# Opening of a streaming-encoder layer: the second half's squares, scales and weight sums moved in a hand-written order, one product taken in whole words for three groups, the first taps later

## Chip, cores and metric

One core of one Trainium2 chip runs the whole layer in one launch. The metric is device microseconds of one execution, median of several. TensorE (PE) does the matrix products, VectorE (DVE) and ScalarE (ACT) prepare their operands and empty their results, GpSimd (POOL) takes a few additions, SyncE (SP) issues most of the transfers.

## The reference, cut to what matters

```
mod = silu(c) @ ada_w + ada_b                      # six rows of 1024: shift, scale, gate, twice
h   = rms_norm(x, g0) * (1 + sc_m) + sh_m          # x: 2048 x 1024, float32
bcv = h @ w_in                                     # 1024 x 3072 -> gate_b, gate_c, v
u   = gate_c * v;  conv = 3 causal taps of u
h   = (gate_b * conv) @ w_out
x   = x + g_m * rms_norm(h, g1)
h   = rms_norm(x, g2) * (1 + sc_f) + sh_f
x   = x + g_f * rms_norm((silu(h@w_g) * (h@w_u)) @ w_down, g3)
```

All is float32. The change lies in the first lines alone: the norm, the modulation and the start of `h @ w_in`.

## The kernel before

**Products.** Every matrix product goes through a Strassen-Winograd step: seven block products P1 to P7 take the place of eight. Their moving operands are built from four quarters of the normalized x, all 128 x 2048: `a` and `b` (tokens 0 to 511, lower and upper half of the channels), `c` and `d` (tokens 512 to 1023). A11 = a (for P1), A12 = b (P2), S3 = e = a - c (P7), S2 = d - e (P6), S1 = c + d (P5), S4 = b - S2 (P3), A22 = d (P4). The stationary operands are 128 x 512 blocks of the weight or sums of two or three of them (`Blocks.sum`).

**Split words.** A float32 operand is split in two fp32r words: ACT casts the high one (`high`, `upper`), DVE subtracts it from the whole to get the low one (`low`, `lower`). One block of 128 contracted channels (a `k`; four to a product) is then three matmuls of 128x512: wh·hi, wl·hi, wh·lo. Below, "a triple".

**Slots.** A phase is a list of slots, one product of one group each (`resident`). In the first phase, in0, groups n = 0, 1, 2 are c, C and b of the first quarter of the channels (gate_c, v and gate_b in the reference come from them); slots 0 to 4 are P1 of n = 0 to 4, 5 to 9 P2 of n = 0 to 4, 10 to 12 P7, 13 to 15 P6, 16 to 18 P5, 19 to 21 P3 and 22 to 24 P4 of n = 0 to 2; then 25 P6, 26 P7, 27 P5 and 28 P3 of n = 3, and so on with n = 4 beside it.

**Order.** Each engine works its instructions in the order in which the program emits them. From slot 13 on a loop emits them slot by slot: `supply` brings weights so many slots ahead (blocks 9, sums 7, high 5, low 4), `events` hold the steps of features, `later(x, f)` puts f x slots on. Slots 0 to 12 are the opening, `start()`, written out by hand: loads of everything first, then the norm factors (`squares`, `factor`/`root`, `spread`, which multiplies by a matrix of ones on PE and copies the result to `rb`), the modulation vectors (`scales`, `shifts`, `turned`, `fold`), the features (`mult` on DVE, `shift` and `upper` on ACT, `lower` on DVE), the products (`products`) and what follows one (`follow`: after P1 an ACT copy c11, after P2 a DVE sum). In the trace's names A12h and A12l are high and low word of A12, r1 is the norm factor of the second 512 tokens, xr their rows of x, v, r1p and r1t steps of its root, in0P a bank of PSUM (left of the arrow) and in3P a pair of weight words (right).

**Accumulators.** A group's P1, P6, P5 and P3 add up in one PSUM bank `pa`, read between them: c11 after P1 and c21 after P6 and c22 after P5, each an ACT copy. So P5 of a group can't start until the copy c21 is through. `taps` (one ACT product and two DVE multiply-adds) and `ready_b` (two DVE products, then `sums` and stores) follow once P3 and P4 of the three groups are there.

**Buffers.** 17 tiles of 128 x 2048 (`big`), 16 raw blocks, 7 weight pairs, 10 temporaries, 8 PSUM banks.

Of the kernel before, what the change touches and what calls it, by code (L numbers as in the profile page):

```python
# [15 lines left out]
P = 128  # L16
# [6 lines left out]
EPS = 1e-6  # L23
# [2 lines left out]
SUBS = ((0, 4), (4, 4), (8, 3))  # L26

LEAD = 3

EARLY = 5  # L30

# [16 lines left out]
def hybrid_conv_layer(  # L48
# [17 lines left out]
    class Engine:  # L66


        def __init__(self, engine):
            self.engine = engine  # L70
# [24 lines left out]
    def pair(name):  # L95
        return pairs.tile([P, 2, CH], F32, tag="wp", bufs=NWP, name=name)
# [306 lines left out]
    class Weight:  # L403


        def __init__(self, kind, grp, op, of, keep=False, ks=None):
            self.kind, self.grp, self.op, self.of, self.keep = kind, grp, op, of, keep
            self.key = (kind, grp, op)
            self.n = width(kind, grp)
            if ks:  # L410
                self.n = len(ks) * P
                self.of = Single(kind, grp, slice(ks[0] * P, (ks[-1] + 1) * P))
            elif of:
                of.split[op] = self
# [16 lines left out]
        def high(self):  # L431
            if self.of:
                self.t = self.of.operand(self.op)
                self.w = pair(f"{self.kind}{self.grp}{self.op}")
                A.copy(self.w[:, 0, : self.n].bitcast(F32R), self.t)

        def low(self):
            if self.of:
                w, n = self.w, self.n
                V.tensor_tensor(w[:, 1, :n].bitcast(F32R), self.t, w[:, 0, :n], ALU.subtract)  # L440
                if self.keep:
                    kept[self.key] = scratch([P, 2, CH], f"k{self.kind}{self.grp}{self.op}")
                    later(2, lambda: A.dma_start(kept[self.key][:, :, :n], w[:, :, :n]))
# [55 lines left out]
    class Group:  # L499
# [72 lines left out]
        def taps(self, u, j, pos):  # L572
            ph = self.ph
            if self.i not in ph.y:
                ph.y[self.i] = big(f"{ph.name}y{self.i}")
            t = ph.y[self.i][:, pos, :]
            w = lambda tap: col(vt, VW + tap * KD + j)

            def rest():
                V.scalar_tensor_tensor(t, u[:, 1 : CH + 1], w(1), t, ALU.mult, ALU.add)  # L580
                V.scalar_tensor_tensor(t, u[:, 0:CH], w(0), t, ALU.mult, ALU.add)

            lag = 0.5 if self.n < LEAD else 1.5
            later(lag, lambda: A.activation(t, u[:, 2:], AF.Copy, scale=w(2)))
            later(lag + (0.5 if self.n < LEAD else 1), rest)

        def ready_b(self, c):
            ph = self.ph
            if c == "12":
                both = (0, self.c11), (2, self.pa)  # L590
            elif c == "21":
                both = (1, self.c21), (3, self.c22)
            else:
                return
            t = ph.y[self.i]
            for pos, src in both:
                V.tensor_tensor(t[:, pos, :], src, t[:, pos, :], ALU.mult)
            own = self.n == len(ph.groups) - 1 and stay[ph.u]
            if c == "12":
                for op, pos in ("A11", 0), ("A12", 2):  # L600
                    if own:
                        later(0.5, partial(own[op][0], t[:, pos, :]))
                        later(1, partial(own[op][1], t[:, pos, :]))
                    else:
                        later(1, partial(store_operands, y_d[ph.u], self.i, (op, t[:, pos, :])))
            if {"12", "21"} <= self.done:
                run(sums(t, y_d[ph.u], self.i, f"{self.name}s", own))


# [259 lines left out]
    for s in slots:  # L869
        ph = s.ph  # L870
        if ph.kind in ("out", "down"):
            w = Weight(ph.kind, s.grp, s.op, None, ks=s.ks)
        elif s.n < LEAD and ph.name != "in0" or ph.name == "in1" and s.g.i == 2:
            w = Weight(ph.kind, s.grp, s.op, None)
        else:
            b = of.setdefault((ph.name, s.n), Blocks(ph.kind, s.grp))
            w = Weight(ph.kind, s.grp, s.op, b, ph.name == "in0" and s.g.i in (1, 2))
        s.w = w
        position.append(len(order))
        order.append(w)  # L880
        if s.n >= LEAD and extra.get(ph.name) and len(position) > 7 * LEAD + 2 * (EARLY - LEAD):
            n = count[ph.name] = count.get(ph.name, 0) + 1
            total = 7 * (len(ph.groups) - LEAD)
            every = 7 * len(in_between[ph.name])
            while extra[ph.name] and every - len(extra[ph.name]) < (0.6 * n if n < total / 3 else n * every / (total - 6)):
                order.append(extra[ph.name].pop(0))
# [7 lines left out]
    def advance(step, to):  # L894
        st = steps[step]
        while st[0] <= to:
            if step in BEFORE:
                advance(BEFORE[step], st[0])
            getattr(order[st[0]], step)()
            st[0] += 1  # L900
# [151 lines left out]
    def start():  # L1052
# [81 lines left out]
        def products(first, ks, ns=range(3)):  # L1134
            for k in ks:
                for n in ns:
                    multiply(slots[first + n], (k,), follow=False)
# [30 lines left out]
        def split(key, op, ks):  # L1168
            for k in ks:
                shift(key, k)  # L1170
                upper(op, k)
                lower(op, k)
# [50 lines left out]
        advance("high", 7)  # L1223
        products(4, range(2, 4), range(1))
        advance("low", 7)
        fold(2)
        shifts(3)
        split("b", "A12", range(2))
        squares(1, range(2, 4))
        dg = factor(1, lambda: [scales(3, i) for i in range(2)])  # L1230
        products(5, range(2), range(1))
        turned(3)
        fold(3)
        follow(0, range(3))
        products(6, range(2), range(1))
        rb[1] = spread(dg, "r1")
        split("b", "A12", range(2, 4))
        products(5, range(2, 4), range(2))
        follow(3, range(2))
        advance("high", 8)  # L1240
        advance("low", 8)
        for k in range(4):
            mult("c", k)
            shift("c", k)
        products(7, range(4), range(1))
        follow(5, range(2))
        advance("high", 9)
        advance("low", 9)
        advance("sums", 12)
        products(8, range(4), range(2))  # L1250


        f.t["e"] = big(f"{ph.name}e")
# [2 lines left out]
            V.tensor_tensor(f.t["e"][:, k, :], f.t["a"][:, k, :], f.t["c"][:, k, :], ALU.subtract)  # L1256
            upper("S3", k)

        for k in range(4):
            e(k)  # L1260
            if k:
                advance("low", 9 + k)
                lower("S3", k - 1)
            if k < 3:
                advance("high", 10 + k)
            if k == 1:
                follow(7, range(1))
            if k == 3:
                follow(8, range(2))
        lower("S3", 3)  # L1270
        products(10, range(2))
        products(10, range(2, 4))
# [15 lines left out]
        follow(10)  # L1288


        for k in range(4):
            V.tensor_tensor(f.t["c"][:, k, :], f.t["c"][:, k, :], f.t["d"][:, k, :], ALU.add)
            upper("S1", k)
        advance("sums", 18)
        advance("high", 18)
        for k in range(4):
            lower("S1", k)
        advance("low", 18)
        for i, step in ((14, f.s4), (15, partial(f.high, "S4")), (16, partial(f.low, "S4")),
                        (17, partial(f.high, "A22")), (18, partial(f.low, "A22"))):  # L1300
            schedule(i, step)

    for ph in phases[1:]:
# [34 lines left out]
    def multiply(s, ks=None, follow=True):  # L1338
        g, op = s.g, s.op
        ks = ks or s.ks  # L1340
        if s.first and op in ("P1", "P2", "P7") and ks[0] == 0:
            t = bank(f"{s.ph.name}{op}_{s.n}")
            setattr(g, {"P1": "pa", "P2": "pb", "P7": "pd"}[op], t)
        acc = {"P2": "pb", "P7": "pd", "P4": "pd"}.get(op, "pa")
        acc = getattr(g, acc)
        hi, lo = s.ph.A[FEATURES[op], s.key]
        begin = s.first and op in ("P1", "P2", "P7")
        last = s.last and ks[-1] == s.ks[-1]
        for k in ks:
            c = slice((k - s.ks[0]) * P, (k - s.ks[0] + 1) * P)  # L1350
            wh, wl = s.w.w[:, 0, c].bitcast(F32R), s.w.w[:, 1, c].bitcast(F32R)
            PE.matmul(acc, wh, hi[:, k, :], start=begin and k == 0, stop=False, skip_group_check=True)
            PE.matmul(acc, wl, hi[:, k, :], start=False, stop=False, skip_group_check=True)
            PE.matmul(acc, wh, lo[:, k, :], start=False, stop=last and k == ks[-1], skip_group_check=True)
        if last and follow:
            g.after(op)
# [64 lines left out]
```

## Time and profile before

| | |
|---|---|
| time, median of 3 runs | 1998.7 us (1995.0 to 1999.45) |
| the profiled execution, its own time | 1995.86 us |
| its span, first to last instruction | 1994.1 us |
| PE busy in the span | 1946.8 us (98%), 8472 matmuls |
| DVE busy | 1467.3 us (74%) |
| ACT busy | 871.1 us (44%) |
| mean granted TensorE clock | 0.992 of full |

The busy share of PE is a mean over the whole run; matmuls are pipelined and their ends are modelled, so a stretch at 10.00 us of 10 is a stretch without a wait, at the clock that was granted in it. The opening has to be read by itself, from the timelines of its engines.

### The profile page before, as it was taken

Reading aid. Unit: us, or ns where it says so; the run is one execution under the profiler, and the core shown is the slowest. Engines: PE = TensorE matmul, PEld = TensorE weight load, DVE = VectorE, ACT = ScalarE, POOL = GpSimd, SP = SyncE. Lnnn points to the kernel's source line nnn. Section 1 sums busy time; section 2 is a strip of 40 time slices with the busy share of each in tenths; the row PEclk is TensorE's granted clock in tenths of the full one; section 3 lists DMA queues with packets and bytes.
Section 4 is the critical chain, followed back from the end, with each engine's and each line's share of the span. In section 5 each row is a group of like instructions: output and inputs, shape, how many; then the busy total and the mean of one; then the engine's idle time right before and its main releaser. Section 6 shows DMA issues by size and latency. Waiting matters only on the chain.

```text
span 1994.1 us, 25033 instructions
## 1 busy us (share of the span) xinstructions
PE 1946.8 (98%) x8472; PEld 1580.3 (79%) x8472; DVE 1467.3 (74%) x2165; ACT 871.1 (44%) x1434; POOL 345.2 (17%) x224
## 2 busy tenths in 40 slices
PE   7799998999999999999999999999999999999998
PEld 3578886777888888888888888888888888888886
DVE  4898778987999876798677755687776665565466
ACT  4533445643434653444333444553333333344452
POOL 0011111310220220144242320120100000011010
PEclk9899999999999999999999999999999999999999
DMA  9349959859996773687566787668565242386644
GB/s 390 119 171 365 330 184 338 308 200 320 313 343 214 288 278 133 195 264 259 180 225 205 262 275 291 230 228 278 184 199 171 101 160 99 106 301 232 198 140 132
DMA packets 204464, 458.98 MB, mean 230 GB/s; under 512 B 22832, under 2 KB 38320, under 8 KB 197936
## 3 DMA queue, kind: packets, MB, share of 16 engines
q1 hardware_dynamic: 176688, 391.98, 57.1%
q10 hardware_dynamic: 27648, 65.41, 8.5%
q8 instruction: 66, 1.08, 0.2%
q14 instruction: 62, 0.51, 0.1%
HBM read 326.23 MB, written 131.07 MB: 229 GB/s over the span
## 4 chain that ended last, share of the span: by engine, by line
PE 73%; DVE 12%; DMA 8%; issue 4%; ACT 2%; ACTq 0%; SPq 0%; POOL 0%; POOLq 0%; DVEq 0%
PE gu1P L76 21%; PE gu0P L76 17%; PE down0P L76 11%; PE down1P L76 9%; PE in0P L76 7%; PE in1P L76 4%; PE out1P L76 4%; DMA ada<-ada_d 1%; DMA in2b<-w_in_d 1%; DVE zz L76 1%; DVE ada L76 1%; DMA kgu0P<-gu0P 1%; DVE xx L76 1%; DVE in1c L76 1%; DVE in0y L76 1%
## 5 line engine op out<-in xcount | busy, mean ns | idle before, releaser
L76 DVE TENSOR_TENSOR gu1a<-gu1P,gu1a 128x512 f32<-128x512 f32 x63 | 43.5, 691 | 108.6 <-PE gu1P L76 108.6
L76 DVE TENSOR_TENSOR gu0a<-gu0P,gu0a 128x512 f32<-128x512 f32 x63 | 43.3, 688 | 71.9 <-PE gu0P L76 69.5
L76 POOL TENSOR_TENSOR gu1a<-gu1a 128x512 f32<-128x512 f32 x11 | 19.0, 1727 | 363.4 <-DVE gu1g11s L76 42.5
L76 POOL TENSOR_TENSOR nq<-nq,nq 128x512 f32<-128x512 f32 x28 | 43.4, 1550 | 144.2 <-ACT nq L76 135.3
L76 ACT COPY gu1a<-gu1P 128x512 f32<-128x512 f32 x42 | 24.7, 588 | 98.6 <-PE gu1P L76 87.4
L76 ACT COPY gu0a<-gu0P 128x512 f32<-128x512 f32 x42 | 24.5, 587 | 84.0 <-PE gu0P L76 82.9
L76 DVE CUSTOM_DVE_ANT_0 ada<-ada,c 128x512 f32<-128x512 f32 x80 | 58.9, 747 | 3.0 <-DMA ada<-ada_d 3.0
L76 ACT COPY gu1g<-gu1P 128x512 f32<-128x512 f32 x24 | 14.1, 589 | 92.9 <-PE gu1P L76 92.9
L76 POOL TENSOR_TENSOR down0q<-down0q,down0q 128x512 f32<-128x512 f32 x14 | 23.9, 1706 | 144.1 <-ACT down0q L76 144.0
L76 POOL TENSOR_TENSOR gu0a<-gu0a 128x512 f32<-128x512 f32 x11 | 18.2, 1658 | 171.5 <-ACT gu0a L76 47.7
L76 ACT COPY gu0g<-gu0P 128x512 f32<-128x512 f32 x24 | 14.1, 588 | 77.1 <-PE gu0P L76 77.1
L76 POOL TENSOR_TENSOR down1q<-down1q,down1q 128x512 f32<-128x512 f32 x10 | 16.1, 1611 | 148.7 <-ACT down1q L76 148.6
L76 DVE TENSOR_TENSOR gu1g<-gu1P,gu1g 128x512 f32<-128x512 f32 x24 | 16.6, 691 | 27.4 <-ACT gu1g L76 26.0
L76 DVE TENSOR_TENSOR down2P<-down2P,down2P 128x512 fp32r<-128x512 f32 x14 | 12.0, 854 | 28.6 <-ACT down2P L76 28.6
L76 ACT ACTIVATE gu1a<-gu1a 128x512 f32<-128x512 f32 x42 | 26.6, 633 | 13.4 <-DVE xo L76 6.0
L76 POOL TENSOR_TENSOR in0y<-in0y 128x512 f32<-128x512 f32 x4 | 5.9, 1465 | 152.7 <-ACT in4P L76 84.7
L76 ACT ACTIVATE gu0a<-gu0a 128x512 f32<-128x512 f32 x42 | 26.6, 632 | 9.9 <-DVE gu0a L76 8.3
L76 POOL TENSOR_TENSOR out1q<-out1q,out1q 128x512 f32<-128x512 f32 x14 | 22.1, 1580 | 50.4 <-ACT out1q L76 50.4
L76 POOL TENSOR_TENSOR out0q<-out0q,out0q 128x512 f32<-128x512 f32 x14 | 22.7, 1618 | 45.6 <-ACT out0q L76 45.5
L76 DVE TENSOR_TENSOR xx<-xx,zz 128x512 f32<-128x512 f32 x32 | 29.1, 908 | 1.1
L76 ACT ACTIVATE nq<-xx 128x512 f32<-128x512 f32 x32 | 20.2, 632 | 19.1 <-DVE xx L76 18.9
L76 DVE TENSOR_TENSOR gu0g<-gu0P,gu0g 128x512 f32<-128x512 f32 x24 | 16.6, 690 | 14.8 <-ACT gu0g L76 13.3
(3231 smaller groups left out, 6750.0 us busy)
## 6 DMA issues: line engine op xcount, KB each, us to landing
ada<-ada_d SPq DMA_DIRECT2D x64, 256.0 KB, 5.3
act0A<-gu0a SPq DMA_DIRECT2D x33, 256.0 KB, 3.5
act1A<-gu1a SPq DMA_DIRECT2D x33, 256.0 KB, 2.9
ada<-ada_d SPq DMA_DIRECT2D x16, 512.0 KB, 9.4
zz<-z SPq DMA_DIRECT2D x32, 256.0 KB, 5.0
xx<-xt_d SPq DMA_DIRECT2D x32, 256.0 KB, 5.2
x<-xx ACTq DMA_DIRECT2D x32, 256.0 KB, 4.8
down0S<-act0S SPq DMA_DIRECT2D x8, 1024.0 KB, 7.0
```

Of the source, the lines that this page charges most:

```text
L76: return tc.keep_in_program_order(f(*args, **kwargs))
```

## The change

Five edits, all before slot 30.

1. **Squares.** The squares of the last two row blocks of the second 512 tokens stand ahead of the fold of the third quarter and of the first split of `b`, on ACT; before they stood behind the split of two of the four parts of `b`. The root `v` of it follows at once on DVE and POOL.
2. **Scales and sums.** The last two `scales` (DVE) are put between the two splits of `b`, the last `fold` ahead of the diagonal, the weight sums of P7 (`sums` 12) ahead of the second half of `b`, the `mult`s of `c` between its splits.
3. **P2 group by group.** P2 of n = 2, 3 and 4 runs one group after the other; before n = 3 and 4 went together, k by k. The sums that follow P2, the weight words of P7 and the parts of `e` and S3 are dealt out anew around it.
4. **Whole words.** P5 of n = 0, 1, 2 takes `c` (which holds S1 then) and the weight block as they are, float32 times float32, one matmul a `k` in place of three: no split of S1 nor of these three weights in the opening. The other nine groups need S1's words; they are made at slots 22 (high) and 23 (low), each in one instruction of 128x2048. S4's subtraction comes forward from slot 14.
5. **Taps.** For n < 3 the ACT product of the taps is 2 slots later, the DVE part 2 slots too, `ready_b` 3 slots.

```diff
+UNSPLIT = {"P5": "c"}
 ...
     def high(self):
             self.t = self.of.operand(self.op)
+            if self.whole_words:
+                return
 ...
-            lag = 0.5 if self.n < LEAD else 1.5
+            lag = 2.5 if self.n < LEAD else 1.5
 ...
         def ready_b(self, c):
+            if self.n < LEAD:
+                later(3, partial(self.gated, c))
+            else:
+                self.gated(c)
 ...
         advance("low", 7)
+        squares(1, range(2, 4))
         fold(2)
         shifts(3)
-        split("b", "A12", range(2))
-        squares(1, range(2, 4))
-        dg = factor(1, lambda: [scales(3, i) for i in range(2)])
-        products(5, range(2), range(1))
+        v = small(4, "v1")
+        V.tensor_scalar(v, sq[1], EPS, None, ALU.add)
+        steps = root(v, "r1")
+        next(steps)
+        shift("b", 0)
+        upper("A12", 0)
+        scales(3, 0)
+        lower("A12", 0)
+        shift("b", 1)
+        upper("A12", 1)
+        scales(3, 1)
+        dg = at_once(steps)
+        lower("A12", 1)
         turned(3)
         fold(3)
-        follow(0, range(3))
-        products(6, range(2), range(1))
-        rb[1] = spread(dg, "r1")
-        split("b", "A12", range(2, 4))
+        dg = diagonal(dg, "r1")
+        products(5, range(2), range(1))
+        rb[1] = spread(dg, "r1")
+        products(6, range(2), range(1))
+        advance("sums", 12)
+        shift("b", 2)
+        upper("A12", 2)
+        mult("c", 0)
+        lower("A12", 2)
+        mult("c", 1)
+        shift("b", 3)
+        upper("A12", 3)
+        lower("A12", 3)
+        follow(0, range(3))
+        mult("c", 2)
+        mult("c", 3)
         products(5, range(2, 4), range(2))
         follow(3, range(2))
-        advance("high", 8)
+        advance("high", 9)
+        follow(5, range(1))
         advance("low", 8)
+        follow(6, range(1))
+        products(7, range(4), range(1))
         for k in range(4):
-            mult("c", k)
             shift("c", k)
-        products(7, range(4), range(1))
-        follow(5, range(2))
-        advance("high", 9)
         advance("low", 9)
-        advance("sums", 12)
-        products(8, range(4), range(2))
+        products(8, range(4), range(1))
+        follow(7, range(1))
+        products(9, range(4), range(1))
 ...
+        e(0)
+        advance("high", 10)
+        e(1)
+        follow(8, range(1))
+        advance("low", 10)
+        lower("S3", 0)
+        advance("high", 11)
+        advance("low", 11)
+        follow(9, range(1))
+        lower("S3", 1)
+        e(2)
+        advance("high", 12)
+        e(3)
+        advance("low", 12)
+        lower("S3", 2)
         lower("S3", 3)
 ...
+        ph.whole = {op: f.t[key] for op, key in UNSPLIT.items()}
         for k in range(4):
             V.tensor_tensor(f.t["c"][:, k, :], f.t["c"][:, k, :], f.t["d"][:, k, :], ALU.add)
-            upper("S1", k)
-        advance("sums", 18)
+            if k:
+                advance("sums", 15 + k)
         advance("high", 18)
-        for k in range(4):
-            lower("S1", k)
-        advance("low", 18)
-        for i, step in ((14, f.s4), (15, partial(f.high, "S4")), (16, partial(f.low, "S4")),
-                        (17, partial(f.high, "A22")), (18, partial(f.low, "A22"))):
+        f.s4()
+        for i, step in ((15, partial(f.high, "S4")), (16, partial(f.low, "S4")),
+                        (17, partial(f.high, "A22")), (18, partial(f.low, "A22")),
+                        (22, partial(f.high, "S1")), (23, partial(f.low, "S1"))):
 ...
+        if s.w.whole_words:
+            for k in ks:
+                PE.matmul(acc, s.w.t[:, k * P : (k + 1) * P], s.ph.whole[op][:, k, :], start=False,
+                          stop=k == s.ks[-1], skip_group_check=True)
```

## Rows read from the trace of the kernel before

**Rows 1.** Busy time of the engines in stretches of the run: the stretch and its length in us, busy us and (instructions) of PE, PE's weight loads, DVE, ACT, POOL, then the granted TensorE clock, the DMA share and GB/s.

```profile
20.00:30.00 10.00, 7.21 (x29) 3.86 (x29) 8.48 (x24) 5.03 (x8) 0.00 (x0) 1.00 1.03 421
46.00:60.00 14.00, 9.40 (x38) 4.60 (x37) 6.96 (x28) 8.78 (x16) 1.38 (x1) 0.94 0.92 369
60.00:66.00 6.00, 6.00 (x16) 4.67 (x17) 4.52 (x8) 4.61 (x8) 0.00 (x0) 0.57 0.00 0
...
88.00:98.00 10.00, 8.24 (x34) 5.93 (x33) 9.90 (x18) 5.96 (x11) 0.00 (x0) 1.00 0.00 0
98.00:104.00 6.00, 4.72 (x14) 3.75 (x15) 5.84 (x8) 2.29 (x3) 0.00 (x0) 0.72 0.29 87
...
130.00:139.00 9.00, 5.53 (x17) 3.79 (x17) 8.86 (x17) 4.14 (x8) 0.71 (x1) 0.81 0.57 230
139.00:200.00 61.00, 61.00 (x269) 50.47 (x270) 51.48 (x73) 20.45 (x36) 17.68 (x12) 1.00 0.96 361
...
1000.00:1100.00 100.00, 100.00 (x443) 82.81 (x442) 71.98 (x90) 36.07 (x64) 33.95 (x23) 1.00 0.64 220
```

**Rows 2.** The chain of work that ended last, in order of time, of the first 200 us: start us, length us, engine and tile.

```profile
51.99 0.17 DVE v L76
...
138.87 61.31 PE in0P L76 x269
```

**Rows 3.** PE's timeline: start us, length us, then the operation, out<-in, the array used, shape, count, and in brackets the idle time before it and what ended it.

```profile
22.27 0.73 PE L76 MATMUL in0P<-in0A11h,in0P 128*128 128x512 f32 x2 [2.13 <-ACT in0A11h L76]
...
56.57 1.12 PE L76 MATMUL r1b<-r1d,one 128*128 128x512 f32 x2 [2.44 <-DVE mB L76]
59.73 1.22 PE L76 MATMUL in0P<-in0A12h,in0P 128*128 128x512 f32 x2 [2.04 <-ACT in0A12h L76]
...
65.02 0.72 PE L76 MATMUL in0P<-in0A12h,in2P 128*128 128x512 f32 x2
...
77.94 0.71 PE L76 MATMUL in0P<-in0S3h,in1P 128*128 128x512 f32 x2 [3.27 <-DVE in0c L76]
...
90.07 0.39 PE L76 MATMUL in0P<-in0S2l,in0P 128*128 128x512 f32 x1
...
95.51 0.39 PE L76 MATMUL in0P<-in0S2l,in2P 128*128 128x512 f32 x1
97.49 0.51 PE L76 MATMUL in0P<-in0S1h,in0P 128*128 128x512 f32 x1 [1.59 <-ACT in0c L76]
99.28 0.76 PE L76 MATMUL in0P<-in0S1h,in0P 128*128 128x512 f32 x1 [1.29 <-DVE in0P L76]
...
108.97 0.62 PE L76 MATMUL in0P<-in0S4h,in0P 128*128 128x512 f32 x2
...
130.50 0.39 PE L76 MATMUL in0P<-in0S3l,in3P 128*128 128x512 f32 x1
133.69 1.22 PE L76 MATMUL in0P<-in0S1h,in3P 128*128 128x512 f32 x2 [2.79 <-ACT in0c L76]
...
138.87 0.74 PE L76 MATMUL in0P<-in0S4h,in3P 128*128 128x512 f32 x2 [0.68 <-ACT in0c L76]
```

**Rows 4.** ACT's timeline, same columns.

```profile
44.97 0.61 ACT L76 CAST in2P<-in2b 128x512 fp32r<-128x512 f32 x1
...
49.77 1.05 ACT L76 ACTIVATE xr<-xr 128x1024 f32<-128x1024 f32 x1
...
60.43 0.62 ACT L76 CAST in0A12h<-in0b 128x512 fp32r<-128x512 f32 x1
60.95 0.58 ACT L76 COPY in0c<-in0P 128x512 f32<-128x512 f32 x1
...
63.90 2.94 ACT L76 ACTIVATE in0c<-in0c,mB,mA 128x512 f32<-128x512 f32 x4 [1.36 <-DVE in0c L76]
...
131.40 0.72 ACT L76 ACTIVATE in0y<-in0C,vt 128x512 f32<-128x512 f32 x1 [2.43 <-DVE in0C L76]
...
133.06 0.58 ACT L76 COPY in0c<-in0P 128x512 f32<-128x512 f32 x1
```

**Rows 5.** DVE's timeline, same columns.

```profile
72.30 0.68 DVE L76 TENSOR_TENSOR in0S3l<-in0e,in0S3h 128x512 fp32r<-128x512 f32 x1
...
78.91 2.48 DVE L76 TENSOR_TENSOR in0d<-in0d,r1r 128x512 f32<-128x512 f32 x4
...
88.54 1.28 DVE L76 TENSOR_TENSOR in0S2l<-in0a,in0S2h 128x512 fp32r<-128x512 f32 x2
...
92.16 1.41 DVE L76 TENSOR_TENSOR in0b<-in0b,in0b 128x512 f32<-128x512 f32 x2
...
96.14 2.49 DVE L76 TENSOR_TENSOR in0S1l<-in0c,in0S1h 128x512 fp32r<-128x512 f32 x4
...
118.78 1.53 DVE L76 SCALAR_TENSOR_TENSOR in0y<-in0c,vt,in0y 128x512 f32<-128x512 f32 x2
```

**Rows 6.** The weight loads of PE's first six matmuls, float32 times float32, 128x128 by 128x512, two loads to a matmul: start us, length us, what ended the idle time before.

```profile
11.82 0.19 PEld L76 LDWEIGHTS wb<-w,one 128*128 128x128 f32 x1 [0.24 <-issue]
12.25 0.19 PEld L76 LDWEIGHTS wb<-w,one 128*128 128x128 f32 x1 [0.24 <-issue]
```

**Rows 7.** The rows of x for the second factor: SP's issue of their four loads, and the time from issue to landing of all eight loads of rows, least, median and most.

```profile
31.37 3.48 SPq L76 DMA_DIRECT2D xr<-x_d  x4
...
DMA to landing us min/median/max: 4.3/8.6/9.9
```

More of the change, by code (lines that the diff above doesn't have):

```diff
@@ L403, in hybrid_conv_layer, with __init__ @@
     class Weight:
-        def __init__(self, kind, grp, op, of, keep=False, ks=None):
+        def __init__(self, kind, grp, op, of, keep=False, ks=None, whole_words=False):
+            self.whole_words = whole_words
             self.kind, self.grp, self.op, self.of, self.keep = kind, grp, op, of, keep
@@ L437, in low @@
         def low(self):
-            if self.of:
+            if self.of and not self.whole_words:
                 w, n = self.w, self.n
@@ L587, in ready_b, with gated @@
         def ready_b(self, c):
+            if self.n < LEAD:
+                later(3, partial(self.gated, c))
+            else:
+                self.gated(c)
+        def gated(self, c):
             ph = self.ph
@@ L605, in ready_b @@
                         later(1, partial(store_operands, y_d[ph.u], self.i, (op, t[:, pos, :])))
-            if {"12", "21"} <= self.done:
+            self.done.add("gated" + c)
+            if {"gated12", "gated21"} <= self.done:
                 run(sums(t, y_d[ph.u], self.i, f"{self.name}s", own))
@@ L876, in hybrid_conv_layer @@
             b = of.setdefault((ph.name, s.n), Blocks(ph.kind, s.grp))
-            w = Weight(ph.kind, s.grp, s.op, b, ph.name == "in0" and s.g.i in (1, 2))
+            w = Weight(ph.kind, s.grp, s.op, b, ph.name == "in0" and s.g.i in (1, 2),
+                       whole_words=ph.name == "in0" and s.n < LEAD and s.op in UNSPLIT)
         s.w = w
@@ L1257, in e @@
             upper("S3", k)
-        for k in range(4):
[L1260 to L1269, printed above, removed]
+        e(0)
[13 more added lines that the diff above has]
+        lower("S3", 2)
         lower("S3", 3)
@@ L1288, in start @@
         follow(10)
+        ph.whole = {op: f.t[key] for op, key in UNSPLIT.items()}
         for k in range(4):
             V.tensor_tensor(f.t["c"][:, k, :], f.t["c"][:, k, :], f.t["d"][:, k, :], ALU.add)
-            upper("S1", k)
-        advance("sums", 18)
+            if k:
+                advance("sums", 15 + k)
         advance("high", 18)
-        for k in range(4):
-            lower("S1", k)
-        advance("low", 18)
-        for i, step in ((14, f.s4), (15, partial(f.high, "S4")), (16, partial(f.low, "S4")),
-                        (17, partial(f.high, "A22")), (18, partial(f.low, "A22"))):
+        f.s4()
+        for i, step in ((15, partial(f.high, "S4")), (16, partial(f.low, "S4")),
+                        (17, partial(f.high, "A22")), (18, partial(f.low, "A22")),
+                        (22, partial(f.high, "S1")), (23, partial(f.low, "S1"))):
             schedule(i, step)
@@ L1345, in multiply @@
         acc = getattr(g, acc)
+        if s.w.whole_words:
+            for k in ks:
+                PE.matmul(acc, s.w.t[:, k * P : (k + 1) * P], s.ph.whole[op][:, k, :], start=False,
+                          stop=k == s.ks[-1], skip_group_check=True)
+            if follow:
+                g.after(op)
+            return
         hi, lo = s.ph.A[FEATURES[op], s.key]
```

## The prediction

> **What bounds the kernel now.** I read the stretches first. Late in the run PE is busy for 100.00 us of 100 at full clock, and from 139 us on for 61.00 of 61 [rows 1]; the chain of waits has one unbroken piece of PE there [rows 2]. So beyond 139 us an instruction on DVE or ACT costs nothing, and whatever brings 138.87 forward brings the end forward, as far as PE's work beyond stays the same. Ahead of it PE loses time in two ways: it stands idle, and after idle stretches it runs at a lower clock (a mean of 0.57 in 60 to 66, 0.72 in 98 to 104, 0.81 in 130 to 139) [rows 1]. Then I read PE's timeline for the places: ahead of r1b and of the second half of P2 (2.44 and 2.04 idle), in P7 (3.27), at the start of P5 (1.59 and 1.29), at P5 of group 3 (2.79), at P3 of group 3 (0.68) [rows 3]. Last I read what DVE and ACT did there: from 78 to 98 DVE is busy for nearly all of the stretch, so there the order and number of DVE's instructions set the time, and PE merely follows [rows 1].
>
> Prices. A triple at full clock: P6 of n = 1 and 2, eight triples, from 90.30 (the start of the triple behind the one at 90.07) to about 95.74 is 5.44, so 0.68 each. At the low clock: four triples from 59.73 to 65.02, 1.32 each. Small DVE work of 128x512 follows itself every 0.60 to 0.62 (the four of 2.48 at 78.91), ACT casts every 0.52, shifts every 0.73, copies every 0.48 (60.95 and its neighbours, an estimate from their 0.58 less the overlap seen in the four shifts) [rows 3 to 5].
>
> **Term 1, from the squares to S3: 6.0 us.** The chain of waits runs through v at 51.99 [rows 2], which waits for ACT's two last squares, behind the two splits of b, at 49.77 [rows 4]. The squares now follow the cast of 44.97 at 45.5. Their rows are there: the last of four issues is out by 34.85, and the longest landing of rows took 9.9, so 44.8 [rows 7]. Two squares with their sums take 2.1; v is at 47.7. From v to r1b it was 4.58 (51.99 to 56.57 [rows 2, 3]) with four scales, the rest of the root, the diagonal and a fold; the same stand in between now, and two lows of b besides, 1.2. Nothing else: ACT makes both highs in 47.6 to 50.4, under it. r1b starts at 53.6, 3.0 earlier, and PE has two triples of P2 and the transposes of the modulation columns to fill part of the wait.
>
> From r1b to the end of b's last high was 4.38 on ACT (to 60.95 [rows 3, 4]); now that is 58.0. Then five copies and two casts (3.4) go ahead of the shifts of c, which start at 61.45 in place of 63.90 [rows 4]. On DVE the three sums of P7's weights and the products of c fill the holes between the lows of b; the last low is at 58.8. P2 of n = 0 and 1 is through at 59.7, and n = 2, 3, 4 follow without a wait, 12 triples, 8.2: 67.9. Behind each DVE takes its sum, and the instruction which waits is that of n = 4: queued behind it on DVE are the low of S3's second part, the last two parts of e, the last weight word of P7 and two lows of S3. Seven instructions and a wait of 0.6 for ACT's cast from 68.0 on: DVE is through with S3 at 72.9, and takes up the products of d there, at 78.91 before [rows 5]. That is the 6.0. PE waits some 1.9 in P7 for the last of its weights, in place of 3.27 [rows 3].
>
> **Term 2, S2 and P6: minus 1.2 us.** From the products of d to S2's last low the order is unchanged: 78.91 to 89.82, 10.9 [rows 5]. It ends at 83.8. PE is done with P7 at 78.3 (12 triples from 67.9 and the wait), so P6 of n = 0 goes as DVE's lows come and ends at 84.2 (90.30 before), n = 1 and 2 at 89.7 (95.74). But PE, which worked on P7 meanwhile, now stands idle here three times, some 0.5, 1.1 and 1.1. An idle 2.13 at 22.27 left the clock of 20 to 30 at 1.00; 1.59 and 1.29 within four microseconds were followed by 0.72 [rows 1, 3]. Bounds: nothing, or four triples at the low clock, 2.5. These three lie between the two cases; I take the middle, 1.2.
>
> **Term 3, P5 in whole words: 2.9 us.** From P6's end at 95.74 to P3 at 108.97 it was 13.2 [rows 3], for twelve triples that need 8.2: waits for S1's lows (2.49 from 96.14) and the weights' [rows 5], and slow clock. Now four sums c + d and six weight sums are left, 2.4 and 4.0 (two take 1.32 [rows 5]): the last c at 88.9, the last weight at 90.2, needed at 96. No wait. A float32 matmul of this shape: its two weight loads are 0.43 apart at full clock, so 0.86 [rows 6], against 0.68 a triple. Twelve: 10.3. So 13.2 - 10.3 = 2.9, although PE's work grows by 2.2.
>
> The row shows 0.86 where the triple takes 0.68, a factor of 1.26. The Trainium skill (FP8 and Floating Point Precision, TensorE Precision Notes) says that true float32 takes four passes through the array; by that, against three for a triple, the factor is 4/3 and twelve cost 10.9, and the sum would be 0.6 smaller. The rule speaks against this edit wherever PE is the bound, and the rows agree in direction.
>
> The words of S1 are made later, for the other groups: one cast and one subtraction of 128x2048, with S4's beside them about 1.9 and 2.3. By adding DVE's instructions from 90.2 on I get S1's low at 116.8; PE wants it at P5 of n = 3, at 121.8. P3 and P4, 24 triples, cover it; if the cover were gone, ACT's and DVE's 4.2 would be on the path. The raw blocks of P5 are held until PE is through with them, 93 to 100; the next loads into such blocks come no later than before.
>
> **Term 4, P5 of n = 3: 4.8 us.** Before, PE stood from 130.73 to 133.69, then ran slow, and P3 came at 138.87 [rows 3]: 8.1, for four triples (2.7) and a copy. The copy c21 it waited for is at 133.06 on ACT, behind the taps' product of 131.40, which itself waited 2.43 for DVE [rows 4]; DVE was two taps and two gates in arrears (1.53 a pair [rows 5]). With the taps 2 slots and the gates 3 slots later, ahead of the copy stand only products of n = 0 and 1 whose inputs are ready about 114 and 120; P6 of n = 3 ends at 119.0. The copy goes at once. What stays is 0.7 for the copy after P5. So 2.7 + 0.7 = 3.4 in place of 8.1: 4.8. The deferred taps and gates (about 5.5 of DVE) come due by slot 27. DVE then lags 3 to 4 behind PE, while weight words are made four slots, 10.9, ahead. Stores of the first y are issued three slots later on SP, so the loads of n = 5 pass in front; nobody waits for these stores yet.
>
> **Sum.** 6.0 - 1.2 + 2.9 + 4.8 = 12.5. The profiled execution took 1995.86, with a span of 1994.1: it becomes 1983.4. It lies 2.84 under the median of the runs, 1998.7; against the median I predict 1986.2, rounded 1986.
>
> **The rivals.**
> - *All of it, as summed*, 1986. With no slow clock in P6, 1985; with the full price and a slow stretch in P2 too, 1989.5: chance 0.62.
> - *Part of it comes back.* The deferred taps and gates meet the next groups' products on DVE, and an ACT copy of n = 4 stands behind a taps' product again; or the second half's chain does not come forward, since a weight block of P7's sums lands late and blocks DVE. Either takes 4.8 to 6.0 back: 1991 to 1992.5. For it: DVE is near full until 139 and runs at 51.48 of 61 thereafter [rows 1]. Against: the slack of 4 slots. 0.22.
> - *The clock falls and stays down through P5.* Twelve float32 matmuls at half clock cost 10.3 more: 1996.5, no change. For it: the idle pieces right before P6. Against: P6's last eight triples run without a wait, and a slow stretch ended after about four triples [rows 3]. The Trainium skill (TensorE: Matmul & The Clock Gate, HAM oscillation) has the same: idle time between bursts throttles the next burst; the traces agree (0.57 after 2.44 and 2.04). 0.06.
> - *The edit does nothing*: the transfers, at a share of 0.96 from 139 to 200 [rows 1], set that stretch's pace and do not come forward. Then PE would wait there for what it gained: 1998.7. Against: they are issued as buffers come free and slots pass, both of which come forward. 0.04.
> - *Slower*, by the same place: if PE, 12.5 ahead, runs into transfers that keep their times, it stands in several pieces, and each piece that slows the clock costs 2.5 beyond the gain. From two such pieces on, the kernel is slower: 1998.7 + 5 = 2004. Nothing shows transfers as last there, PE has no wait in 61 us. 0.06.
>
> **How the numbers follow.** 0.2% of 1998.7, 4 us, is about what a measurement can tell from no change. Faster: the first two, 0.84, and a little of the third: 0.85. Same: 0.09. Slower: 0.06. The range: the median itself may sit 3.7 under, as the lowest run does (1995.0), so 1981; upward it takes in the second rival, 1993. That leaves out 0.16 above and little below.
>
> **What would show it.** Squares at 45.5 on ACT, r1b at 53.6; the products of d at 72.9; P6 done at 90 to 92; P5 with 24 float32 matmuls' records of 0.43 without a wait; no wait ahead of P5 of n = 3; P3 of n = 3 at 126 in place of 138.87, and no new idle time on PE up to 300. Wrong it would be through a wait on DVE between 60 and 73, a PE wait in slots 28 to 36, or slow P5.

## The result and the profile after

The changed kernel takes 1986.8 us (median of 4 runs, 1986.23 to 1987.5) against 1997.53 for the kernel before (4 runs, 1995.0 to 1999.45): a ratio of 0.9947, 95% interval 0.9935 to 0.9959. The forecast was 1986.0, faster. Its profiled execution took 1987.12 us with a span of 1985.3. One execution in the experiments, of the kernel with P7's weights earlier, took 5223.64 us; the median given there is that of its other five.

Part 1 of the page after, the busy time of each engine, its share of the span and its instructions:

```profile
PE 1942.6 (98%) x8460; PEld 1574.5 (79%) x8460; DVE 1464.4 (74%) x2159; ACT 869.7 (44%) x1428; POOL 345.1 (17%) x224
```

The stretches of after, columns as in [rows 1]:

```profile
46.00:60.00 14.00, 12.25 (x50) 6.71 (x49) 12.03 (x36) 9.98 (x19) 1.38 (x1) 1.00 0.92 369
60.00:66.00 6.00, 6.00 (x28) 4.85 (x28) 5.54 (x10) 6.00 (x12) 0.00 (x0) 1.00 0.00 0
...
74.00:78.00 4.00, 4.00 (x12) 3.17 (x11) 4.00 (x8) 2.56 (x4) 0.00 (x0) 0.57 1.02 418
78.00:82.00 4.00, 4.00 (x19) 3.05 (x17) 2.82 (x5) 2.56 (x6) 0.00 (x0) 1.00 0.26 83
82.00:86.00 4.00, 2.69 (x9) 1.27 (x8) 3.98 (x7) 1.75 (x3) 0.00 (x0) 1.00 0.00 0
...
92.00:104.00 12.00, 12.00 (x33) 5.97 (x32) 10.36 (x12) 7.37 (x10) 0.00 (x0) 1.00 0.32 88
...
120.00:130.00 10.00, 9.02 (x40) 7.17 (x39) 9.86 (x18) 3.44 (x6) 0.00 (x0) 1.00 0.57 181
...
139.00:200.00 61.00, 61.00 (x271) 50.53 (x270) 53.77 (x78) 21.52 (x37) 20.48 (x13) 1.00 1.00 373
457.00:487.00 30.00, 24.29 (x99) 19.62 (x98) 19.21 (x33) 9.60 (x17) 0.00 (x0) 0.89 0.96 336
```

Against [rows 1], PE gains in 46 to 60 (12.25 busy in place of 9.40), and the slow clock of 60 to 66 is gone (1.00 for 0.57, 28 matmuls for 16). In 139 to 200 PE is busy throughout in both. Of the stretches shown, two run below full clock, 74 to 78 and a piece of 457 to 487.

PE's timeline of after, columns as in [rows 3]:

```profile
55.15 1.10 PE L78 MATMUL r1b<-r1d,one 128*128 128x512 f32 x2 [0.65 <-DVE r1d L78]
...
58.29 0.73 PE L78 MATMUL in0P<-in0A12h,in0P 128*128 128x512 f32 x2 [0.66 <-ACT in0A12h L78]
...
72.92 0.49 PE L78 MATMUL in0P<-in0S3h,in2P 128*128 128x512 f32 x1 [1.79 <-ACT in2P L78]
73.65 0.50 PE L78 MATMUL in0P<-in0S3h,in2P 128*128 128x512 f32 x1 [0.23 <-DVE in2P L78]
...
84.57 0.50 PE L78 MATMUL in0P<-in0S2l,in0P 128*128 128x512 f32 x1 [0.84 <-DVE in0S2l L78]
...
86.38 0.50 PE L78 MATMUL in0P<-in0S2l,in0P 128*128 128x512 f32 x1 [0.85 <-DVE in0S2l L78]
...
92.85 3.59 PE L78 MATMUL in0P<-in0c,in0b 128*128 128x512 f32 x8
96.28 3.60 PE L78 MATMUL in0P<-in0c,in1b 128*128 128x512 f32 x8
99.71 3.60 PE L78 MATMUL in0P<-in0c,in2b 128*128 128x512 f32 x8
...
124.92 0.61 PE L78 MATMUL in0P<-in0S1h,in3P 128*128 128x512 f32 x2
...
128.78 0.73 PE L78 MATMUL in0P<-in0S4h,in3P 128*128 128x512 f32 x2 [0.98 <-ACT in0c L78]
...
479.83 1.22 PE L78 MATMUL in1P<-in1S4h,in6P3k 128*128 128x512 f32 x2 [5.71 <-ACT in1c L78]
```

Line for line against [rows 3]: r1b 0.65 in place of 2.44, the second half of P2 0.66 in place of 2.04, P7 1.79 and 0.23 in place of 3.27; two new gaps in P6; no wait at the start of P5 (1.59 and 1.29 before), none ahead of P5 of group 3 at 124.92 (2.79 before), 0.98 ahead of P3 of group 3 (0.68 before). The last row lies far beyond the opening, where the prediction looked for nothing.

**How the end follows.** Up to ACT's first cast of P2's words no instruction differs, yet that cast is at 43.93 in the profile of before and at 45.57 in that of after. Over all fourteen profiles of this study it lies between 43.9 and 46.5 for the same code; a second profile of before has it at 46.44. What differs up to there is TensorE's clock. A stretch of after, and one of the second profile of before, columns as in [rows 1]:

```profile
15.00:20.00 5.00, 5.00 (x13) 1.57 (x14) 3.83 (x11) 1.20 (x2) 0.00 (x0) 0.66 1.02 413
...
25.00:30.00 5.00, 4.99 (x12) 3.51 (x11) 4.47 (x14) 1.21 (x2) 0.00 (x0) 0.50 1.03 425
```

In the second profile of before the first matmul of P1 starts at 22.26 behind an idle 2.15, as it starts at 22.27 behind 2.13 in the first [rows 3]; there the clock stayed at 1.00, here a slow stretch follows. Of the fourteen profiles eight have a slow stretch behind this idle piece, two have one in 15 to 20 instead, and four have neither: these four have the cast at 43.9 to 44.0. So I measure from this cast. To the second row of P3 of group 3 (P3 means its second row in all distances below, since its first, at 102.75 in after, overlaps the end of P5 in whole words at 103.1) it is 95.52 us in before and 83.78 in after: the opening is 11.7 shorter. From there to the end it is 1854.65 in before and 1855.95 in after, 1.3 longer. The spans differ by 11.7 - 1.6 - 1.3 = 8.8.

### The profile page after: what moved, and what is told of

It is laid out like the page before. It is cut to its first block, busy times and chain, and to the rows that moved or that the text cites. A ratio compares the mean times of both kernels' runs of the same rounds, so it can differ in the third digit from the quotient of the medians.

```text
span 1985.3 us, 24989 instructions
## 1 busy us (share of the span) xinstructions
PE 1942.6 (98%) x8460; PEld 1574.5 (79%) x8460; DVE 1464.4 (74%) x2159; ACT 869.7 (44%) x1428; POOL 345.1 (17%) x224
## 4 chain that ended last, share of the span: by engine, by line
PE 85%; DVE 6%; DMA 4%; issue 2%; ACT 2%; SPq 0%; POOL 0%; POOLq 0%; ACTq 0%; DVEq 0%
PE gu0P L78 21%; PE gu1P L78 21%; PE down0P L78 11%; PE in0P L78 9%; PE down1P L78 9%; PE in1P L78 8%; PE out1P L78 4%; DMA xr<-x_d 1%; PE pms L78 1%; DMA ada<-ada_d 1%; DVE in1c L78 0%; DVE ada L78 0%; DMA zz<-z 0%; DVE in1y L78 0%; DMA y1S<-in1b1s 0%
## 5 line engine op out<-in xcount | busy, mean ns | idle before, releaser
L78 ACT ACTIVATE xr<-xr 128x512 f32<-128x512 f32 (+1 forms) x24 | 18.5, 772 | 15.6 <-DMA xr<-x_d 14.7
```

Of the source, the lines that this page charges most:

```text
L78: return tc.keep_in_program_order(f(*args, **kwargs))
```

## The experiments

Each is compared with the kernel before on the same chip; "opening" is the distance just defined, 95.52 in before and 83.78 in after.

**Edits 1 to 3 alone** (the order):

```diff
-UNSPLIT = {"P5": "c"}
+UNSPLIT = {}
...
-            lag = 2.5 if self.n < LEAD else 1.5
+            lag = 0.5 if self.n < LEAD else 1.5
```

with the old gates and the old order behind P6.

> Edits 1 to 3 alone (squares, scales and sums in the new order, P2 group by group); S1 is split in the opening and the taps stand as before. Theory (the terms add): the products of d come 5.8 us earlier, P6 ends 4.5 earlier, nothing after it changes: 4.5 us faster, 0.9977 of before. Rival (the parts lean on each other): the wait at P5 of group 3 grows by what was won, since DVE is in arrears there, and the gain is under 1.5 us.

1991.14 us, ratio 0.9974 (0.9962 to 0.9987); opening 89.79, 5.7 shorter. The theory holds in the time, 5.2 us by the ratio, but not in saying that nothing changes after P6. From P6's end to P3 it is 11.05 in place of 13.68: PE has no idle time ahead of P5's first matmul, and the clock is full in 92 to 106. And the wait ahead of P5 of group 3 is 3.79 here (2.79 before), so part of what DVE gains is waited for there.

**Edit 4 alone** (whole words): `UNSPLIT` and the order behind P6 of the changed kernel, all else of the kernel before.

> Edit 4 alone (P5 of three groups in whole words, S1's words made at slots 22 and 23). Theory: P5 lasts 10.3 us in place of 13.2, the rest is as before: 2.9 us faster, 0.9985. Rival: DVE, which makes S1's low word of 2.3 us at slot 23, is still late at P5 of group 3; the wait of 2.79 there grows by 2 to 3 us and the gain is under 1 us.

1995.98 us, ratio 0.9992 (0.9983 to 1.0001); opening 94.37, only 1.2 shorter. In between; the ratio's interval reaches 1, so the time alone shows no gain. PE's timeline:

```profile
131.57 1.22 PE L78 MATMUL in0P<-in0S1h,in3P 128*128 128x512 f32 x2 [3.53 <-ACT in0c L78]
...
137.73 0.74 PE L78 MATMUL in0P<-in0S4h,in3P 128*128 128x512 f32 x2 [0.68 <-ACT in0c L78]
```

From P6's end to P3 it is 10.76 in place of 13.68, so 2.9 are won as expected. But the wait ahead of P5 of group 3 grows from 2.79 to 3.53, with more slow clock behind it: 1.7 are lost again where the copy stands behind the taps, the place that the rival named, though it put the growth of the wait at 2 to 3. Alone the edit is worth 1.2; beside edit 5 it is worth 2.7 (openings of 88.98 and 91.67, below), and in the whole 1.8.

**Edit 5 alone** (taps and gates later):

```diff
-            lag = 0.5 if self.n < LEAD else 1.5
+            lag = 2.5 if self.n < LEAD else 1.5
...
+            if self.n < LEAD:
+                later(3, partial(self.gated, c))
```

> Edit 5 alone (taps and gates of the first three groups later). Theory: the copy c21 of group 3 is no longer behind the taps' product on ACT; the wait of 2.79 before P5 of group 3 and the slow clock after it go: 4.3 us faster, 0.9978. Rival: the weight words of that product come from DVE, too, and are as late; then a wait of 1 to 2 us stays and the gain is under 2 us.

1994.4 us, ratio 0.9981 (0.9973 to 0.999); opening 91.67, 3.9 shorter. No wait ahead of P5 of group 3, and from P7's last row of that group to P3 4.36 in place of 8.95. The theory holds.

**The whole without one part.** Each kernel is the changed one with one part undone, by the reverse of the three edits above.

> The changed kernel with edits 1 to 3 undone: whole words and later taps stay. Theory (the terms add): 2.9 + 4.3 = 7.2 us faster than before, 0.9964. Rival (the parts lean on each other): a gain outside 5.5 to 9.

Without edits 1 to 3: 1991.46, ratio 0.9976 (0.9965 to 0.9987); opening 88.98, 5.2 longer than after's. By the ratio it is 4.8 us faster than before where 7.2 were expected, outside the 5.5 to 9: by the time the rival came true, though the opening is 6.5 shorter than before's.

> The changed kernel with edit 4 undone: new order and later taps stay, S1 and the three weights are split in the opening. Theory: 4.5 + 4.3 = 8.8 us faster than before, 0.9956; P5 lasts 13 us again, with its waits and slow clock. Rival: without the opening's splits of S1 on DVE and ACT being removed the later steps lag too, and the gain is under 7.

Without edit 4: 1989.79, ratio 0.996 (0.9947 to 0.9972); opening 85.56, 1.8 longer. By the ratio it is 8.0 us faster than before, near the 8.8 expected. P5's waits are back, but not its slow clock (1.00 from 92 to 106): from P6's end to P3 it is 12.67, and 10.76 in after.

> The changed kernel with edit 5 undone: taps and gates of the first three groups as early as before. Theory: the wait before P5 of group 3 is back with its slow clock, 4.5 + 2.9 = 7.4 us faster than before, 0.9963. Rival: S1's low word at slot 23 now stands behind taps and gates on DVE, so the wait is longer than the 2.79 of before, 5 to 6 us, and the gain is 4 to 5.

Without edit 5: 1989.25, ratio 0.9959 (0.9947 to 0.9972); opening 87.82, 4.0 longer. By the ratio it is 8.2 us faster than before, for 7.4 expected. PE waits 2.32 ahead of P5 of group 3 and 2.05 ahead of P3; the rival's 5 to 6 in one place was not seen.

Alone the parts give 5.7, 1.2 and 3.9, a sum of 10.7 of 11.7; taken out of the whole they cost 5.2, 1.8 and 4.0, a sum of 11.0. By the ratios alone it is 5.2 + 1.6 + 3.8 = 10.6 us, each term known to about 2 us. So the sums agree, but the parts do work on one another. The order alone wins 2.6 between P6's end and P3, where edit 4 was to win, and loses 1.1 at group 3, where edit 5 wins. From P6's end to P3 edit 4 brings 2.9 alone, 1.9 in the whole, and 0.3 beside the order without the later taps (11.05 without it, 10.76 with it).

**The whole with P7's weights earlier.** The wait of 1.79 in P7 is for the last weight word; here its cast and subtraction go ahead of P2's third sum:

```diff
-        advance("high", 11)
-        advance("low", 11)
+        advance("high", 12)
+        advance("low", 12)
         follow(9, range(1))
         lower("S3", 1)
         e(2)
-        advance("high", 12)
         e(3)
-        advance("low", 12)
```

> The changed kernel with the weight words of P7 of n = 2 made ahead of the sum after P2 of n = 4 and ahead of the third part of e. Theory: the wait of 1.79 us in P7 is what slowed the clock after it (74 to 78), and the late end of P7 held the third weight pair of P6, which cost DVE 1.2 us: without the wait no slow stretch in P7, P6 ends 1 to 2 us earlier, 1 to 2 us faster than the changed kernel, 0.9939 of before. Rival: PE then finishes P7 earlier and stands idle before P6 instead, the clock falls there, and the time is that of the changed kernel, 0.9947, or up to 1 us more.

1986.38 us, ratio 0.9941 (0.9928 to 0.9953); opening 82.04. PE's timeline:

```profile
79.00 1.07 PE L78 MATMUL in0P<-in0S2h,in0P 128*128 128x512 f32 x2 [2.52 <-ACT in0S2h L78]
81.53 0.80 PE L78 MATMUL in0P<-in0S2l,in0P 128*128 128x512 f32 x1 [0.16 <-DVE in0S2l L78]
83.34 0.50 PE L78 MATMUL in0P<-in0S2l,in0P 128*128 128x512 f32 x1 [0.36 <-DVE in0S2l L78]
```

The wait of P7 is gone and PE, through sooner, waits 2.52 ahead of P6 instead; the slow clock moves there too (0.65 in 78 to 82). The same kernel once more:

> P7's weight words first, beside the changed kernel on one chip. From its first profile, 1.75 us less from P2's words to the second triple of P3 of group 3: 1 to 2 us faster than the changed kernel. Rival: no difference, as in the medians of the first comparison (1986.4 and 1986.9).

1987.37 us, ratio 0.9943 (0.993 to 0.9955); opening 82.79. The two profiles have 1.7 and 1.0 off the opening, but the ratios' intervals contain after's. The rival holds: no difference in time that these runs can tell.

**The changed kernel again, and the kernel before again.**

> The changed kernel once more, for the same chip and the same runs of before as the three others: 10.6 us faster than before, 0.9947. Its opening up to the squares is the same program as before; if the 1.6 us by which it came later in the profile are chance of the transfers, this profile has them otherwise.

1986.93 us, ratio 0.9947 (0.9935 to 0.996); opening 83.79, the rest 1857.27. Its stretches from 74 to 90:

```profile
74.00:78.00 4.00, 4.00 (x19) 3.34 (x18) 4.00 (x8) 3.72 (x6) 0.00 (x0) 1.00 0.87 327
78.00:82.00 4.00, 3.18 (x12) 1.64 (x10) 4.00 (x8) 2.43 (x5) 0.00 (x0) 1.00 0.17 54
82.00:86.00 4.00, 3.03 (x9) 2.17 (x10) 4.00 (x8) 1.12 (x3) 0.00 (x0) 0.83 0.00 0
86.00:90.00 4.00, 4.00 (x15) 3.14 (x15) 3.93 (x7) 1.10 (x4) 0.00 (x0) 0.75 0.00 0
```

The program and its waits are the same as after's (1.79 and 0.23 in P7, 0.85 and 0.84 in P6), but the clock falls in P6 here and not in P7.

> The kernel before, once more. Its profiled execution started the words of P2 at 43.93 and took 1854.65 from the second triple of P3 of group 3 to the end of its span; the eight other profiles of this study start those words at 43.9 to 45.6 and take 1855.4 to 1858.5 for the rest. Theory: both are chance of the execution, and this profile has the words at 44.0 to 45.6 and a rest of 1855 to 1858.5. Rival: the change gives back 1.3 us or more later on; then the rest is under 1855 again.

1994.72 us; opening 95.61, the rest 1850.85. The opening repeats to 0.1. The rest was expected at 1855 or more, and the rival came true: it is 5 to 6 us shorter than the whole change's rest (1855.95 and 1857.27). That the gain itself is given back there isn't shown: the two profiles of before lie 3.8 apart, and edit 4 alone, whose opening is only 1.2 shorter, has a rest of 1855.89. PE's timeline there, of this kernel:

```profile
487.98 0.74 PE L76 MATMUL in1P<-in1S4h,in6P3k 128*128 128x512 f32 x2 [1.43 <-ACT in1c L76]
```

> The changed kernel beside the two others: 10.6 us faster than before, 0.9947; from P2's words to the second triple of P3 of group 3 83.8 us, as in both its profiles, wherever the slow stretch of the clock falls.

1986.89 us (1986.36 to 1988.11), ratio 0.9944 (0.9932 to 0.9955); opening 83.49, the rest 1856.34. PE waits 5.89 at the place of 1.43.

**The whole with P2 of n = 3 and 4 together** (edit 3 undone, the rest of the change kept):

```diff
-        products(8, range(4), range(1))
-        follow(7, range(1))
-        products(9, range(4), range(1))
+        products(8, range(4), range(2))
...
+        for k in range(4):
+            e(k)
+            if k:
+                advance("low", 9 + k)
+                lower("S3", k - 1)
+            if k < 3:
+                advance("high", 10 + k)
+            if k == 1:
+                follow(7, range(1))
+            if k == 3:
+                follow(8, range(2))
```

> The changed kernel with edit 3 alone undone: P2 of n = 3 and 4 go together again, k by k, and the parts of e, the weight words and the sums stand as before. Theory: c's shifts still start 2.4 us earlier, but the sums after P2 of n = 3 and 4 and the lows of S3 fall back to their old distances, so the products of d lose 2 to 3.6 of the 5.8 us; 2 to 3.6 us slower than the changed kernel. Rival: the squares and scales won all of it, and the grouping of P2 nothing: within 1 us of the changed kernel.

1984.65 us (1983.22 to 1985.41), ratio 0.9931 (0.9919 to 0.9942); no run of it reaches the lowest of after's third set beside it (1986.36). Not 2 to 3.6 slower but 2.2 faster: the theory is wrong in sign, and in these runs this version is faster than both kernels, though the intervals of its ratio and of after's (0.9932 to 0.9955) overlap. Its opening is 81.67, 2.1 shorter than after's. PE's timeline from 66 to 92 has two waits in it:

```profile
71.65 0.70 PE L78 MATMUL in0P<-in0S3h,in1P 128*128 128x512 f32 x2 [2.73 <-DVE in0c L78]
...
82.99 0.50 PE L78 MATMUL in0P<-in0S2l,in0P 128*128 128x512 f32 x1 [0.18 <-DVE in0S2l L78]
```

DVE's timeline in P2 and P7, of this kernel:

```profile
61.03 0.69 DVE L78 TENSOR_TENSOR in3P<-in3b,in3P 128x512 fp32r<-128x512 f32 x1 [0.45 <-ACT in3P L78]
...
65.40 0.69 DVE L78 TENSOR_TENSOR in0P<-in0b,in0P 128x512 fp32r<-128x512 f32 x1 [1.27 <-ACT in0P L78]
...
72.62 2.48 DVE L78 TENSOR_TENSOR in0d<-in0d,r1r 128x512 f32<-128x512 f32 x4
```

and of after:

```profile
62.59 0.69 DVE L78 TENSOR_TENSOR in3P<-in3b,in3P 128x512 fp32r<-128x512 f32 x1 [0.46 <-ACT in3P L78]
...
67.09 0.69 DVE L78 TENSOR_TENSOR in0c<-in0P,in0c 128x512 f32<-128x512 f32 x1 [0.80 <-PE in0P L78]
...
69.81 0.69 DVE L78 TENSOR_TENSOR in0C<-in0P,in0C 128x512 f32<-128x512 f32 x1 [0.23 <-PE in0P L78]
...
72.90 0.69 DVE L78 TENSOR_TENSOR in2P<-in2b,in2P 128x512 fp32r<-128x512 f32 x1 [0.60 <-ACT in2P L78]
...
74.71 2.50 DVE L78 TENSOR_TENSOR in0d<-in0d,r1r 128x512 f32<-128x512 f32 x4
...
82.02 0.69 DVE L78 TENSOR_TENSOR in0S2l<-in0a,in0S2h 128x512 fp32r<-128x512 f32 x1 [1.20 <-ACT in0S2h L78]
```

The reader is to see how DVE is stopped: group by group it waits for PE at each sum and then for ACT, 2.1 in four pieces, against 1.7 in two. From the cast the products of d come after 28.61 here and after 29.14 in after. And PE, which has more of P7 before it at that time, works on it while DVE makes S2, so that P6 has one gap of 0.18 in place of 0.84 and 0.85. Its slow stretch is there as well (0.79 from 70 to 78, behind the wait of 2.73), but under DVE's chain, which runs on without a wait: from the products of d to P6's end it takes 16.86, as before (16.83), where after takes 18.14.

## Why the prediction was right, step by step

**Term 1, 6.0: right in size, wrong in whom it credited.** From the cast to the products of d it was 34.98 and is 29.14, 5.8. The first half is as forecast: r1b comes 3.1 earlier (3.0 said). The second half was laid to all three edits together, P2 group by group among them. The kernel with P2 by twos shows, in its one profile, that edits 1 and 2 make the whole of it, and half a microsecond more without edit 3. The step that failed is that the last sum costs DVE one wait of 0.6: it costs 0.80 and 0.23 besides, for PE's groups.

**Term 2, minus 1.2: right in size, by another way.** It is -1.3 in after (18.14 against 16.83), -1.65 and -1.3 in its two repeats. Forecast were three gaps in P6 of 0.5, 1.1 and 1.1 and a clock that falls behind them. There are two of 0.84 and 0.85. That the clock may stay full behind such pieces was read from the idle 2.13 at 22.27; behind the same piece it fell in eight of the fourteen profiles, so this bound rested on a chance. In after the clock falls in P7, behind the waits of 1.79 and 0.23 (0.57 from 74 to 78). P7 so ends late and holds the weight pair that ACT's third cast for P6 wants; ACT's timeline of after:

```profile
78.78 0.62 ACT L78 CAST in1P<-in1b 128x512 fp32r<-128x512 f32 x1
80.84 0.62 ACT L78 CAST in2P<-in2b 128x512 fp32r<-128x512 f32 x1 [1.44 <-DVE in0P L78]
81.37 1.14 ACT L78 CAST in0S2h<-in0a 128x512 fp32r<-128x512 f32 x2
```

S2's highs stand behind that cast and DVE waits 1.20 for them at 82.02, so S2, from the products of d to the row of its last two lows, takes 10.93 and not 9.63 as in before. The row names DVE's subtraction of 80.13, but in the second run the same cast goes at 78.16, without a wait, ahead of that subtraction (78.98) and right behind PE's last matmul of P7 with the first group's words (through at 78.00 there, at 80.76 in after): it is PE that holds the pair. In that second run, with the clock full in P7, S2 takes 9.63 and the slow stretch lies on P6 instead. One slow stretch costs 1.3 to 1.65 at either place; only edit 3 undone puts it where it costs nothing.

**Term 3, 2.9: right in time, too much of it credited to edit 4.** P6's end to P3 was 13.68 and is 10.76. But the order alone brings it to 11.05, and without edit 4 the rest of the change brings it to 12.67: the 13.2 that the term starts from holds for the old order only. What P5 waited for there was not S1's lows, as the prediction has it (its 2.49 is busy time of DVE), but the copy c21 behind a weight's cast (1.59) and a weight's low word (1.29) [rows 3]. Twelve float32 matmuls stand without a wait from 92.85 to 103.1, 0.857 each (3.43 from one row of eight records, four matmuls, to the next), at full clock: the 0.43 of [rows 6] twice. By the Trainium skill's four passes (FP8 and Floating Point Precision, TensorE Precision Notes), an estimate worked out from the triple gives 0.91; the row decides. The gain counts in full only if the next wait, at P5 of group 3, is gone too: alone it was 1.2.

**Term 4, 4.8: 4.3.** No wait ahead of P5 of group 3, as forecast. Ahead of P3 0.98 in place of 0.7:

```profile
122.40 0.59 ACT L78 COPY in0c<-in0P 128x512 f32<-128x512 f32 x1 [3.84 <-PE in0P L78]
...
127.63 0.62 ACT L78 CAST in4P<-in4b 128x512 fp32r<-128x512 f32 x1 [3.29 <-DVE in4b L78]
128.15 0.58 ACT L78 COPY in0c<-in0P 128x512 f32<-128x512 f32 x1
```

The copy at 128.15 now stands behind a cast that waits 3.29 for a sum of DVE's. That is the second rival in small: a copy behind another group's work, at a price of 0.3, and gone in the repeats (0.68). The other 0.2 lies in the forecast's own sums: 8.1 less 3.4 is 4.7 and not 4.8, and its 3.4 leaves out 0.16 between the pitch of P5's last triple and the end of its last matmul (128.78 less 0.98 is 127.80, and the last row starts at 127.41 with a pitch of 0.23).

**Sum.** 5.8 - 1.3 + 2.9 + 4.3 = 11.7 for 12.5.

**What the sum left out.** It took the rest for unchanged, since beyond 139 us an instruction on DVE or ACT was to cost nothing. But PE does wait there, in the kernel before already: in its two profiles the waits of 0.3 us and more beyond P3 of group 3 add up to 14.6 and 12.9 us, one of them this, in the first output stage:

```profile
315.62 0.83 PE L76 MATMUL out0P<-out0A120h,out2P 128*128 128x512 f32 x2 [2.79 <-ACT out2P L76]
```

In the three profiles of the changed kernel they add up to 18.0, 18.5 and 18.0. "PE has no wait in 61 us" was right, and the chain of after has one piece of PE from 128.78 to 265. But the fourth rival's transfers are there, 300 us later. ACT's timeline of after:

```profile
470.01 0.36 ACTq L78 DMA_DIRECT2D kgu0P<-gu0P  x1
...
478.16 0.62 ACT L78 CAST gu1P<-gu1b 128x512 fp32r<-128x512 f32 x1 [6.99 <-DMA kgu0P<-gu0P]
478.68 0.61 ACT L78 CAST in1P<-in1b 128x512 fp32r<-128x512 f32 x1
479.20 0.58 ACT L78 COPY in1c<-in1P 128x512 f32<-128x512 f32 x1
```

A pair of weight words can't be written again until its store is through. The store issued at 470.01 is what the cast waits 6.99 for, at a DMA share of 0.96, and the copy of c that PE wants stands behind the cast. PE waits 5.71 at 479.83, and the clock falls once (0.89 in 457 to 487). The chain of waits has the same in before, start and length in us:

```profile
478.33 7.23 DMA kgu0P<-gu0P
...
485.64 0.63 ACT gu1P L76
```

and in the third run of the changed kernel:

```profile
470.71 8.01 DMA kgu0P<-gu0P
...
478.80 0.63 ACT gu1P L78
```

So the store bounded before too, with a wait of PE of 3.46, and of 1.43 in its second profile. The cast behind it came forward by 7.5 where PE had come forward by 10.1 at 129 us: PE waits for the difference. The distance between the first matmuls of the two output stages, which holds this place, is 335.7 to 337.0 in the three profiles of the changed kernel and 333.8 and 330.6 in the two of before: 2 to 6 us more pass there. In all profiles of kernels with an edit the wait is between 3.7 and 6.6, but not in the order of how far they are ahead: the order alone, 5.7 ahead, waits 3.71, edit 4 alone, 1.2 ahead, 4.15, the whole without the order 6.32. What makes the store late in one kernel more than in another wasn't tried.

**The median.** The forecast took 2.84 from the span's execution to the median; for before it is 1.7 to 3.6 (1995.86 and 1994.72 profiled, medians of 1997.5 to 1998.3), for after nothing (1987.12 and 1986.8). So 1986 came out although the profiled execution was 3.7 slower than the 1983.4 forecast: 0.8 of this is the sum, 1.6 the late start, 1.3 the rest. That the missing distance to the median made up for most of it is luck. Between profiles the gain is 8.8, between medians 10.7. Why the other runs of before lie above its profiled ones leaves no row in any trace, and stays open.

**The rivals.** The slow clock through P5 didn't come (1.00 from 92 to 104). The edit that does nothing, and the slower kernel, named a mechanism that the traces show at another place, and at too high a price: 2 to 6 us in place of all 12.5 or several pieces.

## What to carry to other kernels

Look at what a reordered piece makes an engine wait for in the middle, not only at when its last input is ready: a sum taken after each group stops the engine that sets the pace at every group. When a stall is removed, add what the next stall on the path takes back (2.9 became 1.2 alone), and look past the stretch where the gain arises for the next place where the transfers are full. Start the measurement at an instruction up to which both kernels are the same: a slow stretch of the clock ahead of it moves everything behind it, here by up to 2.6 us. And undo one part at a time: a sum that comes out can hide parts that took each other's gains.

## What the hardware showed

- The same program with the same waits had its slow stretch in P7 in two profiles (0.57 and 0.67 from 74 to 78) and in P6 in one (0.83 and 0.75 from 82 to 90). The Trainium skill (TensorE: Matmul & The Clock Gate, HAM oscillation) has idle time between bursts throttle the next one; these rows agree that a slow stretch follows idle time, and show that the rows don't tell which idle piece it will follow: behind 1.79 and 0.23 the clock stayed full in the one run, behind 0.84 and 0.85 in the others. The idle piece of 2.1 ahead of P1 was followed by full clock in four profiles and by a slow stretch in eight, at 0.50 from 25 to 30 in the second profile of before.
- What a slow stretch costs depends on what lies beside it: 1.3 to 1.65 when PE's work in it, or a buffer that PE holds, is next on the path, and nothing measurable when DVE's chain is (16.86 against 16.83).
- With transfers at a share of 0.96, the store of one 128x512 pair issued at 470.01 held its buffer until 478.16.
